# A decoder layer with expert retrieval: sums of key-score pairs on GpSimd, rows of one token tile by transposes, and the first norm's scale and shift in a later stage

## The chip, the cores and the metric

One core of a Trainium2 chip runs the whole layer in one program. The metric is the device time of that program in microseconds; the comparison is between medians of repeated runs.

## The reference

The layer works on 512 tokens with 1024 features. A mixer (pooling heads and latent attention) gives `mix`; then come two norms and a retrieval over 16384 experts. What the change touches is this (reference, cut):

```python
x  = layer_norm(ALPHA * x + g1 * mix, ln1_g, ln1_b)
h2 = x * (1.0 + sc2) + sh2
q  = (h2 @ w_peer_q).reshape(T, 8, 2, 128)            # 8 heads, two halves
sc = einsum('thpd,hpnd->thpn', q, peer_keys)          # 128 keys per half
s1, i1 = top_k(sc[:, :, 0], 16)
s2, i2 = top_k(sc[:, :, 1], 16)
cand = s1[..., :, None] + s2[..., None, :]            # sums of pairs
s, j = top_k(cand, 16)
u = peer_u[idx]; a = gelu(einsum('thkd,td->thk', u, h2))
ffn = einsum('thk,thkd->td', softmax(s) * a, peer_v[idx])
x = layer_norm(ALPHA * x + g2 * ffn, ln2_g, ln2_b)
```

## The kernel before, in words

The tokens stand in four tiles of 128 (t = 0 to 3). For tiles 0 to 2 the expert layer is computed densely over all experts: 128 **u steps** of 24 matmuls each (128 experts, three matmuls per product, since a 32-bit float is split into a high and a low half), and 128 **v steps** of 18 matmuls. Tile 3 is sparse: for each of its 128 choices a gather on the GpSimd queue (L1150) fetches one row of `peer_u` (later of `peer_v`) per token, and one VectorE instruction uses it (L1159 for u, L1172 for v, L1170 for the first v). This is the generator `sparse`.

The order of every engine's instructions is the order in which the program is written; no scheduler moves them. The stages are: mixer; first norm and transposes of h2 (`mix`, `transpose_h2`); **score stage**, the loop over m = 0 to 15 of `peer_scores`; a stage that prepares indices and gates (`top_second`, `g_tiles`); **V stage**, the loop over j = 0 to 127 of v steps with the rest of the u steps and of `sparse` between them; the end (`finish`).

*Score stage.* Iteration m multiplies h2 by the query weights `jpq[m]` in 24 matmuls (PE, L196 to L198), then multiplies the queries of m - 1 by the keys (8 matmuls, L906) and copies the scores out (ScalarE, L909). `weights` prepares the next iteration's weights: ScalarE rounds them to the high half (L208), and the low half is a subtraction, on VectorE for m up to 3 (L205) and on GpSimd after that (L203). The third matmul of an iteration (L198) is the first that reads the low half. VectorE runs `top_first(m - 1)`: the best 16 of 128 for four tiles, five operations each (L883 to L891), and at every second m `top_pairs(h)`: 16 small sums (L927) and the best 16 of the 64 pairs. In some iterations PE has matmuls of `mod_pe` (L314, L326) for the vector g2 in between. In the first four iterations `rows_out` finishes the norm of one tile on GpSimd: times gain (L778), plus bias (L779), a store of the row to DRAM (`x1d`, L780), and for tile 3 also h2 in rows (L783, L784), which `sparse` reads.

*V stage.* Per j, `v_prep` makes the halves of one block of `peer_v` (ScalarE L1214, VectorE L205) and of its weights W. After it come the steps of `sparse` that are due: `ns` counts them against a target that grows with the u and v steps done. After that, 18 matmuls. The buffers called F (17 of 128 x 1024) serve the weights, their halves, gathers and rows alike. A buffer's next user waits for its last reader.

Of the kernel before, what the change touches and what calls it, by code (L numbers as in the profile page):

```python
# [14 lines left out]
AF = mybir.ActivationFunctionType  # L15
# [5 lines left out]
P = 128  # L21
D = 1024
S = 512
NT = S // P
# [22 lines left out]
DT = 3  # L47
# [102 lines left out]
def trace(ctx: ExitStack, tc: tile.TileContext, A, out):  # L150
# [25 lines left out]
    def row(dt=F32, n=S):  # L176
        return T("S2", [P, n], dt)

    def wide(dt=F32, shape=(P, D)):
        return T("F", shape, dt)  # L180
# [9 lines left out]
    def f(t):  # L190
        return t.bitcast(F32)
# [73 lines left out]
    ident = cst[:, C_ID:C_ID + P]  # L265
# [73 lines left out]
    mods = {}  # L339
# [402 lines left out]
    xn = []  # L742
# [19 lines left out]
    for _ in mg:  # L762
        pass

    lnr = []
    hh_t = [T("H", [P, 4, S], F32R) for _ in range(2)]
    hl_t = [T("H", [P, 4, S], F32R) for _ in range(2)]
    h2h = [hh_t[k // 4][:, k % 4] for k in range(KD)]
    h2l = [hl_t[k // 4][:, k % 4] for k in range(KD)]
    x1d = [dram.tile([P, D], F32, name=f"x1d{t}") for t in range(NT)]  # L770
    h2r = {}

    def rows_out(t, xn):
        if not lnr:
            for j in range(2):
                lnr.append(wide())
                sync.dma_start(lnr[j], A["lnr"][j:j + 1].to_broadcast([P, D]))
        pool.tensor_mul(xn, xn, lnr[0])  # L778
        pool.tensor_add(xn, xn, lnr[1])  # L779
        pool.dma_start(x1d[t], xn)  # L780
        if t >= DT:
            h2r[t] = wide()
            pool.tensor_mul(h2r[t], xn, mods["sc2"])  # L783
            pool.tensor_add(h2r[t], h2r[t], mods["sh2"])  # L784

    def transpose_h2(t, xn):
        ts = slice(t * P, t * P + P)
        full = wide(shape=(P, KD, P))
        for q in range(2):
            tp = bank("tp", 2, (P, 4, P))  # L790
            for k in range(4):
                pe.transpose(tp[:, k], xn[:, (4 * q + k) * P:(4 * q + k + 1) * P], ident)
            for k in range(4):
                kk = 4 * q + k
                a, b = modc[:, 2, kk:kk + 1], modc[:, 3, kk:kk + 1]
                act.activation(full[:, kk], tp[:, k], AF.Identity, bias=b, scale=a)
            dve.tensor_copy(hh_t[q][:, :, ts], full[:, 4 * q:4 * q + 4])
            dve.tensor_sub(hl_t[q][:, :, ts], full[:, 4 * q:4 * q + 4], f(hh_t[q][:, :, ts]))


    back, bf = {}, [None]
# [43 lines left out]
            pass  # L845
        return nu[0] > n

    prev, normed = None, []
    ueng[0] = None
    for t in range(NT):  # L850
        if t >= 2:
            load_to(ju[t - 1])
        if t == 3:
            split_to(ju[1] + 1)
        last = prev
        for _ in mixes.pop(t, None) or mix(t, lambda: transpose_h2(*last), xn):
            pass
        prev = (t, xn.pop())
        normed.append(prev)
    for _ in range(2):  # L860
        u_step()
    split_to(ju[2] + 1)
# [4 lines left out]
        u_step()  # L867


    sc = []  # L870
    v16, i16, sv16, pos16 = [], [], [], []
    for t in range(NT):
        if t % 2 == 0:
            vi = wide(shape=(P, 2, 2, PH, 2, TOPK))
        v16.append(vi[:, 0, t % 2])
        i16.append(vi[:, 1, t % 2].bitcast(U32))

        sv16.append(v16[t][:, :, 0])
        pos16.append(v16[t][:, :, 1].bitcast(U32))
# [32 lines left out]
    def top_first(m):  # L912
        top16([(v16[t][:, m // 2, m % 2], i16[t][:, m // 2, m % 2], sc[m][:, t]) for t in range(NT)])

    def top_pairs(h):

        cd = (row() if h < 7 else wide())[:, :NT * 64].rearrange("p (t c) -> p t c", t=NT)
        for t in range(NT):
            for o, a0, na, nb in ((0, 0, 1, 16), (16, 1, 3, 8), (40, 4, 4, 4), (56, 8, 8, 1)):
                dst = cd[:, t, o:o + na * nb].rearrange("p (a b) -> p a b", a=na)  # L920
                s1 = v16[t][:, h, 0, a0:a0 + na].unsqueeze(2).to_broadcast([P, na, nb])
                s2 = v16[t][:, h, 1, 0:nb].unsqueeze(1).to_broadcast([P, na, nb])
                if na == 1:
                    dst, s1, s2 = dst[:, 0], s1[:, 0], s2[:, 0]
                if nb == 1:
                    dst, s1, s2 = dst[:, :, 0], s1[:, :, 0], s2[:, :, 0]
                dve.tensor_add(dst, s1, s2)  # L927
        top16([(sv16[t][:, h], pos16[t][:, h], cd[:, t]) for t in range(NT)])

    g2 = mod_pe(5 * D, "g2", dst=g2r)  # L930
    for m in range(16):
        peer_scores(m)
        if m < NT:
            rows_out(*normed[m])
        next(g2, None)
        if m:
            top_first(m - 1)
            if m % 2 == 0:
                top_pairs(m // 2 - 1)
    u_step()  # L940
    flush()
    u_step()
    top_first(15)
    top_pairs(7)
    sb_front.close()
    ps_front.close()
# [201 lines left out]
    def gather(table, k):  # L1148
        g = wide()
        pool.indirect_dma_start(out=g, out_offset=None, in_=table, in_offset=bass.IndirectOffsetOnAxis(ap=cidx[:, k:k + 1], axis=0))  # L1150
        return g

    def sparse():
        q = [gather(A["u"], k) for k in range(AHEAD - 1)]
        for k in range(P):
# [3 lines left out]
            dve.scalar_tensor_tensor(g, g, 1.0, h2r[DT], op0=ALU.mult, op1=ALU.mult, accum_out=aT[:, k:k + 1])  # L1159
            yield  # L1160
        act.activation(aT, aT, AF.Gelu)
        q = [gather(A["v"], k) for k in range(AHEAD - 1)]
        dve.tensor_mul(aT, aT, g3)
        y3 = T("Y", [P, D])
# [106 lines left out]
    for j in range(NK):  # L1271
# [7 lines left out]
        while np_[0] < j + 2 + (LAST - 1) * max(0, j + 1 + RAMP - NK) // (RAMP - LAST):  # L1279
            v_prep(np_[0])  # L1280
            np_[0] += 1
        while ns[0] < ns0 + (2 * P - ns0) * (j - 2 + nu[0] - nu0) / NJ:
            ns[0] += 1
            if next(side, 1):
                break
# [34 lines left out]
```

## Time and profile before

| | us |
|---|---|
| median of 3 runs (lowest, highest) | 1594.21 (1592.51, 1597.26) |
| profiled execution, its own time | 1597.79 |
| span of its instructions | 1595.9 |
| score stage, from its first matmul to the next u step | 125.51 |
| from there to the end of VectorE's work on scores | 24.73 |
| stage of indices and gates, to the first v matmul | 265.31 |
| V stage, to the last gap of PE | 877.22 |

The profiled execution took 1.9 us more than its span. Times within it are from the start of the span. PE is TensorE, DVE is VectorE, ACT is ScalarE, POOL is GpSimd, SP is the engine that issues most DMAs. A row of a timeline gives start, length, engine, source line, operation, what it writes and reads, and in brackets the idle time of that engine before it and what ended it. The granted clock of TensorE is given as a share of its full 2.4 GHz, so that 0.5 is 1.2 GHz.

### The profile page before, as it was taken

How to read it: one execution, taken by the hardware profiler on the slowest of the kernel's cores; microseconds unless marked ns; L12 is line 12 of the kernel's file. 1: busy time of each engine (PE TensorE's matmuls, PEld its weight loads, DVE VectorE, ACT ScalarE, POOL GpSimd, SP SyncE). 2: the span in 40 equal slices, each digit the busy share in tenths (PEclk: the TensorE clock that was granted, in tenths of full speed). 3: DMA queues.
4: the chain of work that ended last, by engine and by line, in shares of the span. 5: the costliest groups of instructions: out<-in, count | busy, mean ns of one | idle time of the engine just before them, and what ended most of it. 6: DMA issues, size and time to landing. Idle time of an engine off the chain costs nothing.

```text
span 1595.9 us, 22580 instructions
## 1 busy us (share of the span) xinstructions
PE 1504.0 (94%) x8217; PEld 1294.2 (81%) x8217; DVE 1248.0 (78%) x2717; ACT 591.4 (37%) x909; POOL 408.7 (26%) x315
## 2 busy tenths in 40 slices
PE   5999999799888989889999999999999999999996
PEld 4666678578877778769999988888888889898984
DVE  5666467689999999867687787787778778778797
ACT  3344444223333544433343333333333333333342
POOL 0001100633200000023344333342333333333313
PEclk9999999999999999989999999999999999999998
DMA  8655203443224545699889888989989889988881
GB/s 316 232 174 183 86 27 120 172 140 97 80 93 172 185 176 195 227 291 341 305 292 328 310 309 315 324 291 342 313 288 346 283 310 332 323 307 307 292 298 68
DMA packets 147296, 382.70 MB, mean 240 GB/s; under 512 B 11313, under 2 KB 62545, under 8 KB 144113
## 3 DMA queue, kind: packets, MB, share of 16 engines
q1 hardware_dynamic: 109328, 243.56, 44.2%
q0 software_dynamic: 37856, 137.70, 24.3%
q8 instruction: 64, 1.05, 0.3%
q14 instruction: 48, 0.39, 0.1%
HBM read 351.86 MB, written 29.36 MB: 239 GB/s over the span
## 4 chain that ended last, share of the span: by engine, by line
PE 67%; DVE 23%; DMA 4%; issue 2%; ACT 2%; POOL 2%; SPq 0%; DVEq 0%; POOLq 0%; ACTq 0%
PE acc L197 10%; PE acc L198 10%; PE acc L196 10%; PE a L198 9%; PE a L196 9%; PE a L197 9%; DVE F L1083 3%; DVE F L205 3%; DVE F L1087 3%; PE ps L198 2%; PE ps L197 2%; PE ps L196 2%; DVE F L1089 2%; DMA F<-in_v 1%; PE ps L671 1%
## 5 line engine op out<-in xcount | busy, mean ns | idle before, releaser
L205 DVE TENSOR_TENSOR F<-F,F 128x1024 fp32r<-128x1024 f32 (+2 forms) x274 | 334.4, 1221 | 89.6 <-ACT F L236 31.7
L198 PE MATMUL a<-H,F 128*128 128x384 f32 (+1 forms) x1040 | 355.3, 342 | 20.7 <-DVE F L205 18.4
L196 PE MATMUL a<-H,F 128*128 128x384 f32 (+1 forms) x1040 | 360.6, 347 | 2.5 <-ACT F L236 2.4
L197 PE MATMUL a<-H,F 128*128 128x384 f32 (+1 forms) x1040 | 352.1, 339 | 0.0
L1150 POOL DMA_INDIRECT F<-in_u,cidx x128 | 161.0, 1258 | 531.9 <-ACT W L1216 277.0
L196 PE MATMUL acc<-F,W 128*128 128x512 f32 x696 | 271.8, 391 | 14.2 <-ACT W L1216 14.2
L197 PE MATMUL acc<-F,W 128*128 128x512 f32 x696 | 273.3, 393 | 0.1
L198 PE MATMUL acc<-F,W 128*128 128x512 f32 x696 | 273.3, 393 | 0.0
L198 PEld LDWEIGHTS a<-H,F 128*128 128x128 f32 x1040 | 197.3, 190 | 28.1 <-DVE F L205 24.7
L1150 POOL DMA_INDIRECT F<-in_v,cidx x128 | 149.4, 1167 | 271.5 <-DVE F L205 173.2
L196 PEld LDWEIGHTS a<-H,F 128*128 128x128 f32 x1040 | 198.2, 191 | 7.4 <-ACT F L236 3.1
L1172 DVE SCALAR_TENSOR_TENSOR Y<-F,a,Y 128x1024 f32<-128x1024 f32 x127 | 162.8, 1282 | 51.7 <-DMA F<-in_v,cidx 50.2
L197 PEld LDWEIGHTS a<-H,F 128*128 128x128 f32 x1040 | 197.8, 190 | 4.2
L1159 DVE SCALAR_TENSOR_TENSOR F<-F,F 128x1024 f32<-128x1024 f32 x128 | 153.5, 1220 | 54.2 <-DMA F<-in_u,cidx 54.1
L1214 ACT ACTIVATE F<-F 128x1024 fp32r<-128x1024 f32 x128 | 134.9, 1054 | 146.1 <-DMA F<-in_v 67.1
L196 PEld LDWEIGHTS acc<-F,W 128*128 128x128 f32 x696 | 131.2, 189 | 39.8 <-ACT W L1216 14.7
L198 PEld LDWEIGHTS acc<-F,W 128*128 128x128 f32 x696 | 130.9, 188 | 27.9 <-DVE W L205 0.5
L197 PEld LDWEIGHTS acc<-F,W 128*128 128x128 f32 x696 | 131.0, 188 | 26.5 <-DVE F L205 0.9
L236 ACT ACTIVATE F<-F 128x1024 fp32r<-128x1024 f32 x120 | 126.5, 1054 | 30.5 <-DVE Y L1172 14.2
L829 ACT ACTIVATE B<-a 128x384 f32<-128x384 f32 x122 | 59.4, 487 | 210.9 <-PE a L198 210.9
L1216 ACT ACTIVATE W<-B 128x384 fp32r<-128x384 f32 x110 | 57.7, 525 | 202.9 <-PE acc L197 105.1
L198 PE MATMUL ps<-H,F 128*128 128x512 f32 x176 | 74.3, 422 | 11.5 <-POOL F L203 6.2
(284 smaller groups left out, 2041.6 us busy)
## 6 DMA issues: line engine op xcount, KB each, us to landing
F<-in_ut SPq DMA_DIRECT2D x128, 512.0 KB, 6.3
F<-in_v SPq DMA_DIRECT2D x128, 512.0 KB, 6.5
F<-in_wada SPq DMA_DIRECT2D x48, 512.0 KB, 5.1
Gd<-G SPq DMA_DIRECT2D x24, 1024.0 KB, 4.5
G<-Gd SPq DMA_DIRECT2D x15, 1536.0 KB, 13.2
F<-in_wpq SPq DMA_DIRECT2D x16, 512.0 KB, 4.4
F<-in_wout SPq DMA_DIRECT2D x8, 512.0 KB, 3.7
F<-in_win SPq DMA_DIRECT2D x8, 448.0 KB, 8.7
```

The costliest lines, as they stand in the source:

```text
L196: pe.matmul(o, lh, rh, start=first and i == 0, stop=False)
L197: pe.matmul(o, lh, rl, start=False, stop=False)
L198: pe.matmul(o, ll, rh, start=False, stop=last and i == n - 1)
L205: dve.tensor_sub(lo, src, f(hi))
L236: act.activation(hi, w, AF.Copy)
L829: act.activation(back[i], p, AF.Gelu)
L1083: dve.tensor_mul(rows(o1[:, 2:], 8), one, pairs(g[:, 1:], 8))
L1150: pool.indirect_dma_start(out=g, out_offset=None, in_=table, in_offset=bass.IndirectOffsetOnAxis(ap=cidx[:, k:k + 1], axis=0))
L1159: dve.scalar_tensor_tensor(g, g, 1.0, h2r[DT], op0=ALU.mult, op1=ALU.mult, accum_out=aT[:, k:k + 1])
L1172: dve.scalar_tensor_tensor(y3, g, aT[:, k:k + 1], y3, op0=ALU.mult, op1=ALU.add)
L1214: act.activation(Vhl[j][0], v, AF.Copy)
L1216: act.activation(W[j][0], w, AF.Copy)
```

## The change

Three parts.

1. `rows_out` goes. The unscaled normed rows are stored to `x1d` as soon as a tile's norm is done (GpSimd queue, L854 of the new file). Gain and bias are applied in the V stage, inside `sparse`, between the last u and the first v: two loads of gain and bias, then for each tile a load of the row, a multiplication, an addition and a store, all on GpSimd, one tile per step. The target of `ns` counts 4 steps more.
2. The h2 rows of tile 3 are made in `transpose_h2`, by transposing the 8 blocks of h2 back on TensorE and copying them out on ScalarE.
3. The pair sums are done for two tiles at a time (8 instructions per head where there were 16), on GpSimd for heads 0 to 6, at the even m before the odd m at which their best 16 are taken; those of head 7 stay on VectorE.

```diff
-        pool.tensor_mul(xn, xn, lnr[0])
-        pool.tensor_add(xn, xn, lnr[1])
-        pool.dma_start(x1d[t], xn)
-        if t >= DT:
-            h2r[t] = wide()
-            pool.tensor_mul(h2r[t], xn, mods["sc2"])
-            pool.tensor_add(h2r[t], h2r[t], mods["sh2"])
...
+        if t >= DT:
+            h2r[t] = wide()
+            for q in range(2):
+                tp = bank("tp", 2, (P, 4, P))
+                for k in range(4):
+                    pe.transpose(tp[:, k], full[:, 4 * q + k], ident)
+                act.activation(h2r[t][:, q * S:(q + 1) * S], tp.rearrange("p a b -> p (a b)"), AF.Copy)
...
+        pool.dma_start(x1d[t], prev[1])
...
+    def pair_sums(h, eng):
+        cands[h] = (row() if h < 7 else wide())[:, :NT * 64].rearrange("p (t c) -> p t c", t=NT)
+        for t in range(0, NT, 2):
+            for o, a0, na, nb in ((0, 0, 1, 16), (16, 1, 3, 8), (40, 4, 4, 4), (56, 8, 8, 1)):
...
+                eng.tensor_add(dst, s1.to_broadcast(dst.shape), s2.to_broadcast(dst.shape))
...
         peer_scores(m)
-        if m < NT:
-            rows_out(*normed[m])
         next(g2, None)
         if m:
             top_first(m - 1)
             if m % 2 == 0:
+                pair_sums(m // 2 - 1, pool)
+            elif m > 1:
                 top_pairs(m // 2 - 1)
...
     top_first(15)
+    pair_sums(7, dve)
     top_pairs(7)
...
         act.activation(aT, aT, AF.Gelu)
+        h2r.pop(DT)
+        l1 = [wide() for _ in range(2)]
+        for j in range(2):
+            pool.dma_start(l1[j], A["lnr"][j:j + 1].to_broadcast([P, D]))
+        for t in range(NT):
+            x = wide()
+            pool.dma_start(x, x1d[t])
+            pool.tensor_mul(x, x, l1[0])
+            pool.tensor_add(x, x, l1[1])
+            pool.dma_start(x1d[t], x)
+            yield
+        del l1, x
         q = [gather(A["v"], k) for k in range(AHEAD - 1)]
...
-        while ns[0] < ns0 + (2 * P - ns0) * (j - 2 + nu[0] - nu0) / NJ:
+        while ns[0] < ns0 + (2 * P + NT - ns0) * (j - 2 + nu[0] - nu0) / NJ:
```

How the order of the engines' instructions moves, at two places.

GpSimd in the score stage, before. L203 is the low half of the next weights, the rest are rows_out of tiles 0 to 3:

```order
L779 TENSOR_TENSOR F_1912<-F_1912,F_2260 128x1024
L780 DMA x1d_1768<-F_1912 128x1024
L203 TENSOR_TENSOR F_2442<-F_2268,F_2441 128x1024
L778 TENSOR_TENSOR F_2014<-F_2014,F_2258 128x1024
L779 TENSOR_TENSOR F_2014<-F_2014,F_2260 128x1024
L780 DMA x1d_1769<-F_2014 128x1024
L783 TENSOR_TENSOR F_2484<-F_2014,F_967 128x1024
L784 TENSOR_TENSOR F_2484<-F_2484,F_1325 128x1024
L203 TENSOR_TENSOR F_2516<-F_2335,F_2515 128x1024
L203 TENSOR_TENSOR F_2617<-F_2439,F_2616 128x1024
```

The same queue now. F_2238 and F_2239 hold the best 16 that VectorE found, S is the buffer of the 64 sums, and the L203 behind them is the low half of the weights of iteration 4:

```order
L854 DMA x1d_1769<-F_2017 128x1024
L922 TENSOR_TENSOR S_485_2406<-F_2238 128x2x16
L922 TENSOR_TENSOR S_485_2406<-F_2238 128x2x24
L922 TENSOR_TENSOR S_485_2406<-F_2238 128x2x16
L922 TENSOR_TENSOR S_485_2406<-F_2238 128x2x8
L922 TENSOR_TENSOR S_485_2406<-F_2239 128x2x16
L922 TENSOR_TENSOR S_485_2406<-F_2239 128x2x24
L922 TENSOR_TENSOR S_485_2406<-F_2239 128x2x16
L922 TENSOR_TENSOR S_485_2406<-F_2239 128x2x8
L203 TENSOR_TENSOR F_2418<-F_2278,F_2417 128x1024
L203 TENSOR_TENSOR F_2506<-F_2342,F_2505 128x1024
```

The rows_out work is gone from the queue, and eight sums of a head stand ahead of every second L203; the pattern comes seven times.

GpSimd in the V stage now, from the last gather of `peer_u` on:

```order
L1149 DMA F_10372<-in_u,cidx 128x1024
L1164 DMA F_10440<-in_lnr 128x1024
L1164 DMA F_10441<-in_lnr 128x1024
L1167 DMA F_10444<-x1d_1766 128x1024
L1168 TENSOR_TENSOR F_10444<-F_10444,F_10440 128x1024
L1169 TENSOR_TENSOR F_10444<-F_10444,F_10441 128x1024
L1170 DMA x1d_1766<-F_10444 128x1024
L1167 DMA F_10511<-x1d_1767 128x1024
L1168 TENSOR_TENSOR F_10511<-F_10511,F_10440 128x1024
L1169 TENSOR_TENSOR F_10511<-F_10511,F_10441 128x1024
```

Two more tiles follow in the same way, and only then the first gathers of `peer_v` (F_10555, F_10557, F_10561). Before, these gathers stood right behind the last gather of `peer_u`. The buffers of the two L1164 loads are those of F_10331 and F_10330, halves of a v block that PE reads last in the v step ahead of the u step a_10403.

VectorE at the same place now:

```order
L205 TENSOR_TENSOR F_10505<-F_10394,F_10504 128x1024
L205 TENSOR_TENSOR W_10503<-B_8561,W_10502 128x384
L1226 TENSOR_TENSOR B_8664<-B_8664,G_9702 128x384
L205 TENSOR_TENSOR F_10549<-F_10467,F_10548 128x1024
L205 TENSOR_TENSOR W_10547<-B_8664,W_10546 128x384
L1174 TENSOR_TENSOR a_3936<-a_3936,g_3934 128x128
L1181 TENSOR_SCALAR Y_10560<-F_10555,a_3936 128x1024
L205 TENSOR_TENSOR F_10589<-F_10398,F_10588 128x1024
L1226 TENSOR_TENSOR B_8734<-B_8734,G_9702 128x384
```

L1181 uses the first gather of `peer_v`, F_10555; the low half F_10589 of a u step's weights stands behind it. That u step on PE now:

```order
L196 MATMUL acc_6848<-F_10548,W_10546 128x512
L197 MATMUL acc_6848<-F_10549,W_10546 128x512
L198 MATMUL acc_6848<-F_10548,W_10547 128x512
L196 MATMUL a_10661<-H_1762,F_10588 128x384
L197 MATMUL a_10661<-H_1764,F_10588 128x384
L198 MATMUL a_10661<-H_1762,F_10589 128x384
```

Between the last read of F_10331 and F_10330 and the u step a_10661 stand 144 matmuls on PE: three u steps and four v steps.

## Rows read from the trace of the kernel before

**Rows 1.** Busy time by stretch: limits, length, each engine's busy us (instructions), clock, DMA share, GB/s.

```profile
273.73:399.24 125.51, 113.12 (x542) 90.50 (x541) 102.03 (x731) 30.72 (x45) 57.24 (x27) 0.95 0.44 143
423.97:689.28 265.31, 227.19 (x1969) 203.91 (x1968) 244.19 (x518) 115.77 (x187) 0.00 (x0) 0.95 0.50 175
689.28:1566.50 877.22, 875.90 (x4323) 783.18 (x4321) 682.67 (x862) 317.94 (x429) 316.66 (x259) 1.00 0.88 309
1000.00:1200.00 200.00, 200.00 (x994) 179.70 (x993) 154.94 (x204) 72.26 (x98) 73.95 (x61) 1.00 0.90 312
```

**Rows 2.** Timeline of PE in the score stage.

```profile
284.65 1.05 PE L906 MATMUL ps<-S,S 128*128 128x128 f32 x8
...
298.97 0.80 PE L198 MATMUL ps<-H,F 128*128 128x512 f32 x1 [5.29 <-DVE F L205]
...
321.59 0.79 PE L198 MATMUL ps<-H,F 128*128 128x512 f32 x1 [6.20 <-POOL F L203]
...
350.97 1.05 PE L906 MATMUL ps<-S,S 128*128 128x128 f32 x8
...
357.31 1.05 PE L906 MATMUL ps<-S,S 128*128 128x128 f32 x8
...
364.91 1.05 PE L906 MATMUL ps<-S,S 128*128 128x128 f32 x8
```

**Rows 3.** Timeline of GpSimd ahead of the second of these waits.

```profile
319.19 2.34 POOL L203 TENSOR_TENSOR F<-F,F 128x1024 fp32r<-128x1024 f32 x1
```

**Rows 4.** Chain of work that ended last, VectorE in the score stage: start, us, what.

```profile
348.23 0.76 DVE F L883 x4
...
357.57 1.35 DVE S L927 x16
358.93 0.51 DVE F L883 x4
...
362.28 0.76 DVE F L883 x4
```

**Rows 5.** Timeline of VectorE: start of the first best-16, end of the scores.

```profile
286.49 0.87 DVE L883 MAX8 F<-S 128x8 f32<-128x128 f32 x4 [2.67 <-DMA x1d<-F]
...
423.97 0.20 DVE L1043 CAST iotab<-cst 128x128 bf16<-128x128 f32 x1
```

**Rows 6.** Groups of instructions, GpSimd and VectorE: count, busy us, mean ns, idle before.

```profile
L203 POOL TENSOR_TENSOR F<-F,F 128x1024 fp32r<-128x1024 f32 x18 | 43.0, 2389 | 76.8 <-ACT F L208 31.7 <-issue 12.9 <-PE ps L197 11.2
L203 POOL TENSOR_TENSOR S<-F,S 128x512 fp32r<-128x512 f32 x4 | 5.2, 1314 | 62.3 <-ACT S L208 62.3
L297 POOL COPY cz<-cact 128x8 f32<-128x8 f32 x2 | 0.3, 192 | 0.1
...
L205 DVE TENSOR_TENSOR F<-F,F 128x1024 fp32r<-128x1024 f32 x256 | 315.1, 1232 | 77.4 <-ACT F L236 31.7 <-ACT F L1214 30.4 <-ACT F L208 7.6
```

**Rows 7.** DMA issues: count, KB of one, median us to landing.

```profile
F<-in_v SPq DMA_DIRECT2D x128, 512.0 KB, 6.5
x1d<-F POOLq DMA_DIRECT2D x4, 512.0 KB, 3.1
F<-in_v,cidx POOLq DMA_INDIRECT x128, 7.4
```

**Rows 8.** Timeline of PE at two shorter waits.

```profile
419.71 0.69 PE L198 MATMUL a<-H,F 128*128 128x384 f32 x1 [2.04 <-POOL F L203]
...
560.27 0.45 PE L198 MATMUL a<-H,F 128*128 128x384 f32 x1 [2.23 <-DVE F L205]
```

**Rows 9.** Busy time in short stretches that begin with these waits' ends.

```profile
419.63:423.04 3.41, 3.33 (x10) 3.33 (x11) 3.41 (x36) 0.00 (x0) 0.02 (x1) 0.50 0.02 5
...
560.27:563.70 3.43, 3.43 (x35) 3.18 (x36) 3.40 (x8) 0.60 (x1) 0.00 (x0) 1.00 0.74 306
```

**Rows 10.** Timeline at the transposes of tile 3: PE, ScalarE.

```profile
269.17 0.42 PE L196 MATMUL a<-H,F 128*128 128x384 f32 x1
...
269.32 2.89 ACT L796 ACTIVATE F<-ps,modc 128x128 f32<-128x128 f32 x8
```

More of the change, by code (lines that the diff above doesn't have):

```diff
@@ L763, in trace @@
         pass
-    lnr = []
     hh_t = [T("H", [P, 4, S], F32R) for _ in range(2)]
@@ L771, in trace @@
     h2r = {}
[L773 to L777, printed above, removed]
-        pool.tensor_mul(xn, xn, lnr[0])
-        pool.tensor_add(xn, xn, lnr[1])
-        pool.dma_start(x1d[t], xn)
-        if t >= DT:
-            h2r[t] = wide()
-            pool.tensor_mul(h2r[t], xn, mods["sc2"])
-            pool.tensor_add(h2r[t], h2r[t], mods["sh2"])
     def transpose_h2(t, xn):
@@ L846, in u_step @@
         return nu[0] > n
-    prev, normed = None, []
+    prev = None
     ueng[0] = None
@@ L858, in trace @@
         prev = (t, xn.pop())
-        normed.append(prev)
+        pool.dma_start(x1d[t], prev[1])
     for _ in range(2):
@@ L867, in trace @@
         u_step()
-    sc = []
+    sc, vis, cands = [], [], {}
     v16, i16, sv16, pos16 = [], [], [], []
@@ L874, in trace @@
             vi = wide(shape=(P, 2, 2, PH, 2, TOPK))
+            vis.append(vi)
         v16.append(vi[:, 0, t % 2])
@@ L913, in top_first @@
         top16([(v16[t][:, m // 2, m % 2], i16[t][:, m // 2, m % 2], sc[m][:, t]) for t in range(NT)])
-    def top_pairs(h):
[L917 to L927, printed above, removed]
+    def pair_sums(h, eng):
+        cands[h] = (row() if h < 7 else wide())[:, :NT * 64].rearrange("p (t c) -> p t c", t=NT)
+        for t in range(0, NT, 2):
+            for o, a0, na, nb in ((0, 0, 1, 16), (16, 1, 3, 8), (40, 4, 4, 4), (56, 8, 8, 1)):
+                v = vis[t // 2][:, 0, :, h]
+                dst = cands[h][:, t:t + 2, o:o + na * nb]
+                s1, s2 = v[:, :, 0, a0:a0 + na], v[:, :, 1, 0:nb]
+                if na > 1 and nb > 1:
+                    dst = dst.rearrange("p t (a b) -> p t a b", a=na)
+                    s1, s2 = s1.unsqueeze(3), s2.unsqueeze(2)
+                eng.tensor_add(dst, s1.to_broadcast(dst.shape), s2.to_broadcast(dst.shape))
+    def top_pairs(h):
+        cd = cands.pop(h)
         top16([(sv16[t][:, h], pos16[t][:, h], cd[:, t]) for t in range(NT)])
```

## Prediction

> **What bounds the kernel now.** I read the table of stretches first. In the V stage PE is busy for 875.9 of 877.2 us while DVE is busy for 78% of it [rows 1]: PE sets its length, and work added to another engine costs nothing there unless PE comes to wait for it. In the stage of indices and gates DVE is busy for 244 of 265 us and PE for 227 [rows 1], so that stage starts when DVE is done with the scores (423.97 [rows 5]) and shifts with that moment. The score stage has no single bound: PE 113 and DVE 102 of 125.5 us [rows 1]. Its timelines say what happens in it. Undisturbed, an iteration on PE takes 6.34 us, and a pair 13.94 where matmuls for g2 stand between (L906 at 350.97, 357.31, 364.91 [rows 2]); four such groups and two smaller ones lie in the stage, about 1 us each, so 16 x 6.34 + 6 = 107.4 us, a mean of 13.4 a pair. The stage took 18.1 us more. Two waits of PE explain it: 5.29 us for an L205 whose buffer was held by a row that rows_out had not yet stored, and 6.20 us for an L203 that stood behind rows_out on GpSimd [rows 2, 3]; the remaining 6.6 us are a short wait before them and the slower clock after each. From then on the chain of waits runs on DVE: a pair of iterations costs it 14.05 us, 9.35 for two best-16 (4.67 each), 1.36 for 16 sums, 3.35 for the best 16 of the pairs [rows 4]. DVE is the later of the two by a little, and ends 24.7 us after PE has left the scores.
>
> **Part 1, what is removed and moved in the score stage.** rows_out goes from GpSimd, and the two waits of PE with it: -18.1 us for PE. The stores at L854 are issued before the stage and stand ahead of nothing urgent. The 16 sums leave DVE for heads 0 to 6: -1.36 us a pair for DVE, which would then need 12.7 a pair and no longer bind against PE's 13.4.
>
> **Part 2, transposes.** PE now turns tile 3 back before it may go on to the u step at 269.17. These transposes need ScalarE's eight outputs, 2.89 us from 269.32, ending at 272.2 [rows 10], and about 0.5 us of their own. PE leaves at 272.7 instead of 269.2: +3.5 us. The two copies on ScalarE are hidden; nothing waits for h2 in rows before the V stage. The scores begin at 273.7 + 3.5 = 277.2.
>
> **Part 3, pair sums on GpSimd: a new loop.** This is the first place where I expect a cost. In the new order eight sums stand ahead of every second L203. They wait for DVE's best-16 of m - 1, that waits for the key matmuls, which stand at the end of iteration m on PE; and PE's iteration m + 2 waits for that L203. One turn of the loop, from the third matmul of iteration m to that of m + 2:
>
> - rest of the 24 matmuls after the third: 22 x 0.227 = 5.0 us;
> - key matmuls, copy, start of DVE: 286.49 - 284.65 = 1.84 [rows 2, 5];
> - best-16 of m - 1 on DVE: 4.67 [rows 4];
> - eight sums on GpSimd: X;
> - L203: 2.39 [rows 6], and 0.3 for the hand-overs (PE started 0.06 us after L203's end [rows 2, 3]).
>
> That is 14.2 + X, against 13.4 that PE needs. X has no row. GpSimd takes 1.314 us for 512 columns and 2.389 for 1024 [rows 6], so 2.1 ns a column and 0.24 us an instruction: eight instructions with 256 columns in all give 2.5 us. The lower bound is eight times its smallest copy, 0.192: 1.5; above, I allow 0.5 us each for broadcast operands: 4. I take 2.5, from the same operation. So PE waits about 3 us at every second iteration. Waits of that size were followed by half clock once and not another time (2.04 us, then 0.50; 2.23 us, then 1.00 [rows 8, 9]); being longer here, I count 3.4 us at half clock after each, which delays the matmuls in the loop by 1.5 us. A turn is then 18.2 us.
>
> The Trainium skill (GPSIMD Engine Reference, Engine selection) advises VectorE for two-input elementwise work and gives GpSimd about twice its time. By that estimate, from DVE's 0.7 us for eight sums, X would be 1.4 and the score term below some 8 us better; no run here shows X.
>
> In order: iteration 2 starts at 277.2 + 11.7 (two iterations with one group of key matmuls) and ends 6.34 us later; DVE begins on the scores of m = 1 1.03 us after that (1.84 less the key matmuls' share) and takes 4.67; sums 2.5, L203 and hand-overs 2.6: iteration 4 has its low half at 306.1, where PE would have been at 303.1. Five more turns bring iteration 14, and a sixth the u step behind the scores, whose L203 also stands behind sums: 306.1 + 6 x 18.2 = 415.3. From there 3.7 us for its matmuls, 1.84 for the last scores, then on DVE 4.67, 0.7 (the eight sums of head 7) and 3.35: 429.6 against 423.97, **+6 us**. Without slow clock it is -3; with X of 1.5 in addition -10, with X of 4 and slow clock +16. So the stage, freed of 18 us, is about as long as before: the removed wait is replaced by a new one.
>
> **Part 4, gain and bias in the V stage.** 256 steps become 260; the extra work is off PE and DVE, and 5 MB more in 877 us at 309 GB/s [rows 1] is 2% of the traffic. What counts is the order. GpSimd does load, multiply, add, store for four tiles one after the other and only then issues the first gather of `peer_v`. DVE waits for that gather at L1181, and behind L1181 stands the L205 for a u step (F_10589). From the moment E at which PE frees the two gain and bias buffers:
>
> - both loads and the first row issued at 0.6 us each, the row landing 6.5 us after its issue (the same size in this stage [rows 7]): E + 7.7;
> - two GpSimd operations of 2.39 [rows 6] with gaps 4.9, store 0.6: E + 13.2;
> - three more tiles, each 6.5 + 4.9 + 0.7 = 12.1, the next load being behind the store: E + 49.5;
> - first gather, 7.4 to landing [rows 7]: E + 56.9;
> - L1181 and L205, 2 us at L205's price with the first a little shorter [rows 6]: E + 58.9.
>
> Up to the third matmul of that u step PE has 146 matmuls, at 200 / 994 us each [rows 1] 29.4 us. So PE **stands for 29.5 us**, in a stage where it stood nowhere; with the slow clock after it (2 x 2.85 us followed the two long waits above: 18.1 less 11.5 and 0.9) **+32 us**. Nothing gives it back: the remaining matmuls are as many as before. DVE's own lead covers none of it, since its instructions are in order. The bounds: with every landing at 3.1 us, as the stores in a quiet stage took [rows 7], the gather comes at E + 38 and the cost is +15; with landings of 9 us, +45.
>
> The row's 3.1 us was in a stage with a DMA share of 0.44, and the loads at 6.5 and 7.4 were in one of 0.88 [rows 1, 7]; I go by the latter. The Trainium skill (DMA: Bandwidth & Descriptors, Anatomy of one DMA) gives a DMA from this queue 2.0 us plus its bytes at 436 GB/s, an estimate of 3.2 us for one row tile, and by it the cost would be the lower bound, +15. The stores' 3.1 us agrees with it, the loads of the V stage do not.
>
> **Sum.** +6 and +32 make +38 us. The profiled execution took 1597.8 by its own time, so 1635.8; the median of the runs is 3.6 us lower, which gives **1632 us**. The extremes are -10 + 15 and +16 + 45 on 1594: 1599 to 1655.
>
> **The rivals.**
>
> *The scores gain, the V stage loses* (chance 0.16). If the sums don't hold L203, PE leaves the scores at 277.2 + 107.4 = 384.6 and DVE is done 17.7 us later (a start of 1.0, then two best-16, two of pairs and the last sums), at 402.3: -22. With +32 that is 1604. For it: GpSimd was idle for more than half of that stage [rows 1]. Against it: idle time doesn't help a loop, and even X = 0 leaves 14.2.
>
> *Faster: gain and bias stay hidden, too* (0.07). The same -22 and 0 from the V stage: 1572. It takes GpSimd being through four tiles and a gather within 29.4 us of E, or being 30 us ahead of PE; the first asks for 1 us or less a landing, the second for free buffers that the program hasn't given. The first gather's time against 29.4 us decides.
>
> *No difference* (0.07): the V stage at its lower bound of +15 and the scores at -10 to -20, within 0.3% (4.8 us, about what a measurement here can tell from none).
>
> *Worse than the forecast* (0.08): X near 4, or landings that queue behind three loads at once: above 1650.
>
> **Numbers.** The forecast, both new waits with about their prices, has 0.62, and stretches from 1616 to 1650. To leave out no more than two in ten the range reaches down to the first rival: 1604 to 1650. Slower is 0.62 + 0.16 + 0.08 = 0.86, same 0.07, faster 0.07.
>
> **What would show it.** Right: PE in the V stage shows one idle gap of 20 to 40 us that ends at an L205 or L1181 on DVE, released by the first gather of `peer_v`, and it is the only one; in the score stage PE waits at L198 for GpSimd's L203 at iterations 4, 6, ... 14, some 3 to 5 us each, and the waits behind rows_out are gone; DVE ends the scores within 10 us of 424; PE leaves tile 3's transposes 3.5 us later. Wrong: no gap in the V stage, or eight sums in under 1 us and a score stage that ends 20 us earlier.

## The result, and the profile after

The changed kernel takes 1607.05 us (median of 5 runs, 1605.43 to 1611.10) against 1594.61 us of the kernel before in runs beside it: a ratio of 1.0078, 95% interval 1.0066 to 1.0091. It is 12.4 us slower, where 1632 was forecast: the direction is right, the size is a third. The profiled execution took 1606.82 us by its own time with a span of 1605.1, so 9.2 us over the span of before; it is less than 12.4 because the profiled execution of the kernel before, 1597.79 us, lay 3.2 us above the median of its runs.

Where the 9.2 us are can be read from four moments. In the kernel before they are 423.97 (VectorE done with the scores [rows 5]), 685.54 (first matmul of the V stage), 1582.37 (its last) and 1595.9 (end). Now they are 410.27, 671.71, 1591.84 and 1605.1.

| part | before | after | difference |
|---|---|---|---|
| up to the end of the scores on VectorE | 423.97 | 410.27 | -13.7 (forecast +6) |
| indices and gates, to the first matmul of the V stage | 261.57 | 261.44 | -0.1 |
| V stage, first to last matmul | 896.83 | 920.13 | +23.3 (forecast +32) |
| end | 13.5 | 13.3 | -0.3 |

The table ahead of the prediction cuts the V stage at 689.28 and 1566.50; here it is counted from its first matmul to its last. The busy time by stretch (limits, length, then PE, weight loads, DVE, ACT, POOL with their counts, clock, DMA share, GB/s), cut as in [rows 1], with the end of the score stage in a row of its own:

```profile
277.89:389.19 111.30, 109.04 (x542) 86.54 (x541) 89.70 (x644) 30.49 (x45) 39.31 (x66) 1.00 0.38 118
389.19:410.10 20.91, 18.55 (x102) 17.94 (x101) 19.31 (x138) 8.50 (x12) 11.55 (x8) 0.92 0.26 76
410.10:675.45 265.35, 228.81 (x1992) 205.86 (x1991) 244.99 (x520) 115.92 (x187) 0.96 (x1) 0.96 0.50 175
675.45:1576.50 901.05, 876.90 (x4322) 784.41 (x4320) 684.67 (x862) 317.12 (x429) 348.90 (x277) 0.99 0.88 307
```

PE stood for 12.4 us of the score stage before and stands for 2.3 now; in the V stage it is the reverse, 1.3 us and 24.

**The score stage.** First the timeline of PE, then GpSimd's and VectorE's, over one turn of the loop:

```profile
304.43 0.50 PE L198 MATMUL ps<-H,F 128*128 128x512 f32 x1
...
309.56 1.05 PE L902 MATMUL ps<-S,S 128*128 128x128 f32 x8
...
318.81 0.50 PE L198 MATMUL ps<-H,F 128*128 128x512 f32 x1 [0.20 <-POOL F L203]
...
361.78 0.50 PE L198 MATMUL ps<-H,F 128*128 128x512 f32 x1 [1.33 <-POOL F L203]
...
392.13 0.69 PE L198 MATMUL a<-H,F 128*128 128x384 f32 x1 [2.36 <-POOL F L203]
```

```profile
314.79 1.64 POOL L922 TENSOR_TENSOR S<-F 128x32 f32<-128x32 f32 x8 [7.51 <-DVE F L885]
316.38 2.37 POOL L203 TENSOR_TENSOR F<-F,F 128x1024 fp32r<-128x1024 f32 x1
```

```profile
311.37 0.86 DVE L879 MAX8 F<-S 128x8 f32<-128x128 f32 x4
...
314.22 0.87 DVE L885 MAX8 F<-S 128x8 f32<-128x128 f32 x4
315.00 0.08 DVE L887 MATCH_VALUE_LOAD F<-F,S 128x8 f32 x1
```

The turn is there in the forecast order: third matmul of an iteration (304.43), key matmuls (309.56), VectorE's best 16 (from 311.37), GpSimd's sums (314.79), L203 (to 318.75), third matmul two iterations later (318.81). It takes 14.38 us where the forecast had 18.2, and PE hardly waits: 0.20 us here, later 1.33, 0.38 and 2.36 us. The six turns from 304.43 to 392.13 take 14.62 us on average, four of them 14.3 to 14.4 and the last two 15.1 and 15.2.

**The V stage.** PE's only long gap, and what VectorE did then:

```profile
1149.53 0.69 PE L198 MATMUL a<-H,F 128*128 128x384 f32 x1 [23.91 <-DVE F L205]
```

```profile
1147.59 0.75 DVE L1181 TENSOR_SCALAR Y<-F,a 128x1024 f32<-128x1024 f32 x1 [31.66 <-DMA F<-in_v,cidx]
1148.26 1.22 DVE L205 TENSOR_TENSOR F<-F,F 128x1024 fp32r<-128x1024 f32 x1
```

GpSimd ahead of it: the loads of gain and bias, load and multiplication of the first tile and of the second, the multiplication of the fourth, and the first gather. Additions and stores lie between them.

```profile
1096.35 1.14 POOL L1164 DMA_DIRECT2D F<-in_lnr  x2 [7.00 <-PE acc L198]
1097.47 0.55 POOL L1167 DMA_DIRECT2D F<-x1d  x1
1105.18 2.64 POOL L1168 TENSOR_TENSOR F<-F,F 128x1024 f32<-128x1024 f32 x1 [7.17 <-DMA F<-x1d]
...
1111.37 0.54 POOL L1167 DMA_DIRECT2D F<-x1d  x1
1116.23 2.39 POOL L1168 TENSOR_TENSOR F<-F,F 128x1024 f32<-128x1024 f32 x1 [4.32 <-DMA F<-x1d]
...
1137.01 2.33 POOL L1168 TENSOR_TENSOR F<-F,F 128x1024 f32<-128x1024 f32 x1 [4.31 <-DMA F<-x1d]
...
1142.94 1.00 POOL L1149 DMA_INDIRECT F<-in_v,cidx  x1 [0.30 <-issue]
```

It is the forecast chain, place by place: the buffers come free at E = 1096.35 with PE's last read, PE has 29.27 us of matmuls left (forecast 29.4), and its u step waits for the L205 behind L1181 behind the first gather. The chain takes 53.2 us instead of 58.9.

### The profile page after: what moved, and what is told of

Same layout as the page of the kernel before. It is cut to its first block, busy times and chain, and to the rows that moved or that the text cites. A ratio compares the mean times of both kernels' runs of the same rounds, so it can differ in the third digit from the quotient of the medians.

```text
span 1605.1 us, 22565 instructions
## 1 busy us (share of the span) xinstructions
PE 1499.9 (93%) x8225; PEld 1290.6 (80%) x8225; DVE 1234.8 (77%) x2597; ACT 592.1 (37%) x911; POOL 428.1 (27%) x379
## 4 chain that ended last, share of the span: by engine, by line
PE 52%; DVE 14%; DMA 4%; POOL 1%; issue 1%; ACT 1%; SPq 0%; POOLq 0%; DVEq 0%; ACTq 0%
PE acc L197 10%; PE acc L198 10%; PE acc L196 10%; PE a L198 8%; PE a L196 8%; PE a L197 7%; DVE F L1082 3%; DVE F L205 3%; DVE F L1086 3%; DVE F L1088 2%; DMA F<-in_v 2%; DMA F<-x1d 1%; PE gp L1095 1%; POOL F L1168 1%; POOL F L1169 1%
## 5 line engine op out<-in xcount | busy, mean ns | idle before, releaser
L205 DVE TENSOR_TENSOR F<-F,F 128x1024 fp32r<-128x1024 f32 (+2 forms) x274 | 332.9, 1216 | 86.4 <-ACT F L1225 30.1
L1149 POOL DMA_INDIRECT F<-in_v,cidx x128 | 158.7, 1240 | 240.9 <-DVE F L205 129.4
L196 PEld LDWEIGHTS acc<-F,W 128*128 128x128 f32 x696 | 131.1, 188 | 39.4 <-ACT W L1227 14.2
L1095 PE MATMUL gp<-F 128*128 128x128 bf16 x1152 | 81.8, 220 | 2.0 <-DVE F L1088 1.9
```

The source lines that it names most:

```text
L196: pe.matmul(o, lh, rh, start=first and i == 0, stop=False)
L205: dve.tensor_sub(lo, src, f(hi))
L1095: pe.matmul(p[:, j], o[:, 0, j], o[:, n, j], start=n == 2, stop=n == 1)
```

## The experiments

Kernels of one group ran beside their own runs of the kernel before, whose median lay between 1594.05 and 1597.61. Moments are from the profiled executions. A time without a ratio beside it is that of a single run. "Gap" is a wait of PE.

### The loop in the score stage

**Sums one iteration later.** `pair_sums` goes to the odd m, behind the L203 that PE needs next.

```diff
         if m:
+            if m > 1 and m % 2:
+                pair_sums(m // 2 - 1, pool)
             top_first(m - 1)
-            if m % 2 == 0:
-                pair_sums(m // 2 - 1, pool)
-            elif m > 1:
+            if m > 1 and m % 2:
                 top_pairs(m // 2 - 1)
```

> The changed kernel with the pair sums of a head issued on GpSimd one iteration later, behind the low half of the next weights. Theory (a loop PE - VectorE - GpSimd's sums - low half - PE sets 14.35 us a pair of iterations): the waits of PE at the third matmul of every second iteration go, a pair takes PE's own 13.4, the wait of 2.36 us at the u step behind the scores goes with its slower clock, and VectorE ends the scores at 402 to 406 instead of 410.3; the median falls by 4 to 8 us, the gap in the V stage stays at 24. Rival (VectorE is the bound again, as before the change): VectorE ends within 2 us of 410 and the median stays.

1599.15 us, ratio to before 1.0019 (1.0010 to 1.0029). VectorE ends the scores at 401.94, PE has no wait at an L203 in the score stage, the gap in the V stage stays (23.87). So the order on GpSimd's queue costs the change 8 us.

**Twice the sums.** Each of GpSimd's sums is issued twice.

> The changed kernel with every pair sum on GpSimd done twice (same result). Theory (the eight sums lie in the loop): seven times 1.6 us more ahead of the low half, a pair takes 16 us instead of 14.35, and VectorE ends the scores 9 to 16 us later, more if the clock falls in the longer waits; the time rises by about as much, to 1616 or above. Rival (GpSimd's sums are beside the path): VectorE ends within 2 us of 410 and the time stays at 1607.

1636.34 us; VectorE ends at 436.81, 26.5 us later, and more than expected. PE's waits, and the busy time of the 3.4 us right behind each of the first four:

```profile
306.50 0.80 PE L198 MATMUL ps<-H,F 128*128 128x512 f32 x1 [2.64 <-POOL F L203]
326.31 0.79 PE L198 MATMUL ps<-H,F 128*128 128x512 f32 x1 [2.72 <-POOL F L203]
344.76 0.50 PE L198 MATMUL ps<-H,F 128*128 128x512 f32 x1 [2.66 <-POOL F L203]
361.61 0.50 PE L198 MATMUL ps<-H,F 128*128 128x512 f32 x1 [2.66 <-POOL F L203]
...
378.45 0.80 PE L198 MATMUL ps<-H,F 128*128 128x512 f32 x1 [3.85 <-POOL F L203]
...
398.89 0.80 PE L198 MATMUL ps<-H,F 128*128 128x512 f32 x1 [2.93 <-POOL F L203]
...
418.53 0.69 PE L198 MATMUL a<-H,F 128*128 128x384 f32 x1 [3.97 <-POOL F L203]
```

```profile
306.45:309.86 3.41, 3.35 (x8) 2.68 (x9) 3.41 (x31) 0.00 (x0) 2.33 (x2) 0.50 0.66 184
...
326.30:329.70 3.40, 3.39 (x8) 2.71 (x9) 3.40 (x32) 0.00 (x0) 2.28 (x1) 0.51 0.62 174
...
344.70:348.10 3.40, 3.34 (x15) 2.76 (x16) 3.40 (x31) 0.00 (x0) 2.37 (x2) 1.00 0.11 37
361.60:365.00 3.40, 3.40 (x15) 2.82 (x16) 3.40 (x32) 0.00 (x0) 2.30 (x1) 1.00 0.11 40
```

With 16 sums of 4.2 us instead of 8 of 1.64 a turn takes 19.8 and 18.5 us at first: half clock (0.5 of 2.4 GHz) follows the first two waits. From 344.76 to 361.61, where the clock stays at 1.00, a turn is 16.85, which is 14.38 and the 2.56 us that the sums are longer, to 0.1. Behind each of the last three waits the clock is at 0.50 for 3.4 us, and the last two turns take 20.4 and 19.6 us. Those turns at half clock are the regime that the forecast described; only X has to be 4.2 for it.

**All sums on VectorE**, still for two tiles at a time, at the place of the change:

```diff
-                pair_sums(m // 2 - 1, pool)
+                pair_sums(m // 2 - 1, dve)
```

> The changed kernel with the sums of all heads on VectorE, still for two tiles at a time (8 instructions a head), at the same place of the program. Theory (the turn of 14.35 us runs through GpSimd's sums and the L203 behind them; VectorE alone needs 9.35 + 0.7 + 3.35 = 13.4 a pair): L203 no longer waits for VectorE, a pair of iterations takes 13.4 to 13.6 us, and VectorE ends the scores at 402 to 405, as with the sums one iteration later: about 1600. Rival (VectorE's load is what sets the pace and GpSimd relieves it): VectorE ends 0.7 us a head later than in the changed kernel, at about 415, and the time is 1611 or more.

1602.93 us, ratio 1.0038 (1.0026 to 1.0050). Two iterations take 13.94 us with a g2 group between (L902 at 302.39 and 316.33), as undisturbed before [rows 2]; VectorE ends at 404.82. GpSimd isn't needed for the sums: with half as many instructions (0.90 us for eight, 1.35 for sixteen [rows 4]) VectorE keeps PE's pace.

**Transposes back behind the last two u steps** ahead of the scores (`turn_back` after them, on the kept `full`).

> The changed kernel, with the eight transposes back and their two copies moved behind the last two u steps ahead of the score stage. Theory (PE stands for ScalarE's eight outputs, two waits of 1.39 and 0.74 us, and does nothing else wrong): the waits go, the scores begin at 275 to 276 instead of 277.9, everything behind them is some 2 to 2.7 us earlier: about 1604. Rival (the transposes themselves, about 1 us, are the whole price and the waits only move): the start of the scores stays within 0.7 us of 277.9 and the time within 1 us of the changed kernel's.

The scores begin at 273.94; the waits of 1.39 and 0.74 us at L791 are gone, and VectorE ends at 406.57. The V stage begins 3.2 us earlier (668.53), and the time, 1605.73 us, is 1.3 us below the change's median, which a single run cannot tell from none.

### The gap in the V stage

**All loads first.** The four rows are loaded right behind gain and bias into four buffers, before the first multiplication.

> The changed kernel with the four rows of x1d loaded at once ahead of the first multiplication, so that only the first landing stands in GpSimd's chain. Theory (the gap is GpSimd's chain less PE's 29 us of work): three landings of about 4.9 us with their issue leave the chain, the gap shrinks from 23.9 to 8 to 12 us and the time by as much, to about 1593. Rival (the operations on GpSimd, not the landings, hold VectorE through the port that they share): the gap changes by less than 4 us.

1595.70 us; the gap:

```profile
1138.96 0.69 PE L198 MATMUL a<-H,F 128*128 128x384 f32 x1 [10.03 <-DVE F L205]
```

13.9 us less than in the change, with the same operations and the same bytes: those were the landings of tiles 1 to 3 in a row, 14.3 us in the change.

**Spread over the v half.** One piece (load; multiplication; addition and store) after every fourth v step of `sparse`, so that no gather waits for the chain.

> The changed kernel with gain and bias spread between the v steps of the sparse tile: every fourth step one piece (loads, multiplication, addition and store apart), so that GpSimd never waits for a landing ahead of a gather. Theory (order: VectorE waits for the first gather of peer_v, which stands behind four tiles in GpSimd's queue): the one gap of 23.9 us in the V stage goes, that stage takes 877 to 880 us instead of 901, the median falls by 22 to 25 us to about 1583, 0.7% below the kernel before. Rival (the extra traffic and GpSimd's operations cost the time, wherever they stand): the V stage stays at 895 or more, in many small gaps, and the median above 1600.

1605.76 us, ratio 1.0058 (1.0037 to 1.0079): no better. The long gap is gone, but three waits sum to 10.6 us (3.84 us at 1174.81, 2.65 at 1200.49, 4.11 at 1288.01), and the V stage takes 914.6; with the clock at 0.50 to 0.62 behind each of these waits, PE's busy time is 6.8 us longer as well. My first reading was that a buffer given up by a store still under way held up a low half. **One buffer for all rows**, kept from the first load to the last store, should have ended that:

> The changed kernel with gain and bias in the V stage as in the spread version, but with one buffer for all four rows, one piece at every second step, and a piece left empty between a store and the next load into the same buffer; it starts at the sixth step of the v half. Theory (the spread version lost what it won because a buffer given up by a store still under way went to a low half for PE a few us later, and the gathers behind it were late in turn): with the buffer kept, that can happen only once, after the last store; the waits of PE in the V stage sum to 0 to 4 us, and the stage from its first v matmul to its last comes near the 896.8 us it took before the change (894 to 902): 1582 to 1588. Rival (three buffers less for 100 us or more are the cause): waits like those of the spread version (11 to 12 us in all), about 1598 to 1606.

1603.04 us, ratio 1.0049 (1.0033 to 1.0064); waits of 9.11 us at 1201.48 and 1.49 at 1272.53, V stage 913.2. The reading falls; the time is what the rival, three buffers less, expected. What happened before the 9.11 us, on GpSimd and on VectorE:

```profile
1178.27 2.40 POOL L1174 TENSOR_TENSOR F<-F,F 128x1024 f32<-128x1024 f32 x1
...
1186.00 1.06 POOL L1149 DMA_INDIRECT F<-in_v,cidx  x1 [4.46 <-DVE F L205]
```

```profile
1177.82 3.94 DVE L1191 SCALAR_TENSOR_TENSOR Y<-F,a,Y 128x1024 f32<-128x1024 f32 x1
...
1196.72 1.28 DVE L1191 SCALAR_TENSOR_TENSOR Y<-F,a,Y 128x1024 f32<-128x1024 f32 x1 [8.02 <-DMA F<-in_v,cidx]
```

L1191, else 1.28 us, took 3.94 beside GpSimd's L1174. And the next gather was issued only when a VectorE instruction had freed a buffer, so that its landing lay open. Two more kernels, which leave gain and bias out of the computation, part the two: **without the operations** (loads, stores and held buffers stay) and **the operations alone** (on one buffer of zeros, no loads or stores).

> The spread version with one row buffer, without its eight operations on GpSimd: gain and bias are left out of the computation, rows are loaded and stored unchanged, and the three buffers are held just as long. If the missing buffers are what costs in the spread versions: PE waits in the V stage for about 11 us as with the operations. If the operations are (a VectorE instruction that meets one of them takes up to 2.7 us longer, the gathers behind it are late in turn): 0 to 2 us of waits, and a V stage of 894 to 898 us.

> The spread version with one row buffer, with its eight GpSimd operations on a buffer of zeros at the same places: no loads, no stores, one buffer held instead of three; gain and bias are left out of the computation. If the buffers and DMAs are what costs: 0 to 2 us of waits of PE in the V stage, which takes 894 to 898 us. If the operations are: 8 to 12 us of waits as in the spread version.

Without operations: one wait of 5.83 us, the others 0.53 or less, V stage 906.7, 1594.64 us. Operations alone: one of 1.67 us, V stage 899.4, 1587.06 us. Against the 896.8 of before, buffers and DMAs cost 9.9 us, the operations 2.6, and both together 16.4. Buffers and DMAs are the larger part, but not the whole. That the two do more than add is not shown: each length is from one execution, and the operations on zeros, with a single input buffer, took 16.1 us in all where those of the version with one row buffer took 20.9.

**In the stage of indices**, where GpSimd has nothing to do [rows 1] and buffers can be spared (a piece at every second step of `g_tiles`):

> The changed kernel with gain and bias in the stage of indices and gates, one piece (load; multiplication; addition and store) at every second step of it, instead of in the V stage. Theory (what costs in the V stage is only that the first gather of the v rows stands behind a chain of landings): the gap of 23.9 us in the V stage is gone with nothing in its place, since no F buffer is held there and GpSimd has nothing to do in the stage of indices; that stage grows by 0 to 3 us; VectorE ends the scores near 410 as before: 1582 to 1587. Rival (GpSimd's eight operations of 2.4 us share the memory port with VectorE, which sets the pace of that stage): the stage grows by up to 19 us, from 265 to 280 or more, and the time is 1597 to 1602.

1602.55 us, ratio 1.0037 (1.0026 to 1.0047). The V stage is down to 894.1 with no gap, but the stage of indices takes 284.7 instead of 261.4 us. VectorE and GpSimd there:

```profile
471.64 0.68 DVE L1099 TENSOR_TENSOR F<-F,gp 128x1024 bf16<-128x1024 bf16 x1
472.24 2.84 DVE L1103 TENSOR_TENSOR F<-iotab,sm 128x1024 bf16<-128x1024 bf16 x1
475.01 2.56 DVE L1105 TENSOR_TENSOR F<-F,gp 128x512 bf16<-128x512 bf16 x1
```

```profile
472.18 2.35 POOL L1079 TENSOR_TENSOR F<-F,F 128x1024 f32<-128x1024 f32 x1 [6.58 <-DMA F<-x1d]
474.61 2.67 POOL L1081 TENSOR_TENSOR F<-F,F 128x1024 f32<-128x1024 f32 x1
```

Operations of 0.68 and 0.42 us take 2.84 and 2.56, each until GpSimd's is over. GpSimd's eight operations, 21.3 us in all, add 17.7 us to VectorE's busy time in that stage (241.1 to 258.8); the other 5.5 us are idle time of VectorE whose cause is not shown. The rival holds, with 23 us where it had 19: the stage in which GpSimd was idle is the dearest place. The Trainium skill (SBUF — State Buffer, SBUF: two separate sides) says that VectorE and GpSimd share one port pair as an exclusive lock, held for a whole instruction; this trace agrees: L1103 and L1105 end 0.5 and 0.3 us after the operations that they met.

**At the end.** The rows are loaded once, for the second norm, and GpSimd multiplies and adds in that buffer:

```diff
     def load_ln2(ts):
...
+        for t in ts:
+            pool.tensor_mul(x1s[t], x1s[t], ln2[2])
+            pool.tensor_add(x1s[t], x1s[t], ln2[3])
```

> The changed kernel with gain and bias at the end of the program instead of in the middle of the V stage: rows are loaded once, as they are for the second norm anyway, and GpSimd multiplies and adds in that same buffer (tile 3 after the last gather, tiles 0 to 2 while the last v steps run); the four extra loads and four stores of rows are gone, two buffers more are held for some 30 us. Theory (the gap is only the first gather behind the chain; GpSimd is idle after its last gather at 1541 and VectorE uses the rows from 1561 and 1579 on): no gap in the middle of the V stage, the stage takes 894 to 899 us, the tail is 0 to 4 us longer: 1582 to 1587. Rival (buffers, as in the spread versions, or VectorE waiting for the rows of tile 3, or the last norms waiting for GpSimd's six operations at the end): waits of 5 us or more in the last 60 us, 1590 or more.

1598.85 us, ratio 1.0016 (1.0004 to 1.0027). No gap until 1549; then eight waits between 0.2 and 2.4 us, 13.3 in all, beside GpSimd's operations, as VectorE's timeline there shows:

```profile
1549.51 2.70 DVE L205 TENSOR_TENSOR B<-B,B 128x384 fp32r<-128x384 f32 x1
1552.13 0.55 DVE L1216 TENSOR_TENSOR B<-B,G 128x384 f32<-128x384 f32 x1
1552.60 3.59 DVE L205 TENSOR_TENSOR F<-F,F 128x1024 fp32r<-128x1024 f32 x1
```

An L205 of 0.55 us takes 2.70, one of 1.22 takes 3.59: the rival again, and these rows point to the port rather than to the buffers, though the two were not parted here.

**Quarters from one buffer.** One buffer holds 256 columns of gain, of bias and of a row tile; a piece at every third step over most of the v half, 32 operations on 256 columns.

```diff
+            gb = wide(shape=(P, 4, D // 4))
+            g, b, x = gb[:, 0], gb[:, 1], gb[:, 2]
+            for c in range(4):
+                cs = slice(c * D // 4, (c + 1) * D // 4)
...
+                for t in range(NT):
+                    pool.dma_start(x, x1d[t][:, cs])
+                    yield
+                    pool.tensor_mul(x, x, g)
+                    pool.tensor_add(x, x, b)
+                    pool.dma_start(x1d[t][:, cs], x)
+                    yield
```

> The changed kernel with gain and bias in the V stage, worked off in quarters of 256 columns from one buffer that holds a quarter of the gain, of the bias and of one row tile; one piece (load; or multiplication, addition, store) at every third step, so over most of the v half. Theory (in the spread versions two missing buffers more and VectorE instructions held up to 2.7 us by an operation of 2.4 us made the remaining waits): one buffer is held instead of three and each operation is a quarter as long, so PE's waits in the V stage sum to 0 to 2 us and the stage takes 895 to 899 us: 1583 to 1588, about what the run with the operations alone took (1587). Rival (32 more DMAs on GpSimd's queue and 32 operations hold up the gathers): waits of 5 us or more, 1592 or more.

1586.03 us, ratio 0.9947 (0.9925 to 0.9968). V stage 899.2, waits of PE 0.98, 0.35 and 0.53 us: as expected, and what the operations alone took. The operations are shorter and the buffers fewer at the same time; which of the two did it was not parted.

### All three edits

Sums one iteration later and transposes behind the u steps, with gain and bias in the stage of indices, spread with one row buffer, at the end, or in quarters:

> The three edits together: sums on GpSimd one iteration later, transposes back behind two u steps, gain and bias in the stage of indices. Theory (three separate waits, whose prices add): 1607 less 8 (sums), less 2 to 3 (transposes), less 21 to 25 (gain and bias) = 1571 to 1576, 18 to 23 us faster than the kernel before. Rival (what is gained ahead of the stage of indices is lost in it, or GpSimd's work there slows VectorE): 1585 or more.

> The same, and with it the sums on GpSimd one iteration later and the transposes back behind the last two u steps. Theory (the three waits are separate): 1607 less 8 less 2 less 20 to 24: 1573 to 1578. Rival (buffers): 1587 or more.

> The same, with the sums on GpSimd one iteration later and the transposes back behind the last two u steps. Theory (three separate waits): 1607 less 8 less 2 less 20 to 25 = 1572 to 1577, 1.1 to 1.4 per cent faster than the kernel before. Rival (as for gain and bias at the end alone): 1580 or more.

> The same, with the sums on GpSimd one iteration later and the transposes back behind the last two u steps. Theory: 1583 to 1588 less 8 less 1 to 3 = 1573 to 1578, about 1.2 per cent faster than the kernel before. Rival: as for the version in quarters alone, or the wait of 5.2 us that came at the start of the stage of indices in the earlier versions with all three edits: 1579 to 1583.

1591.17, 1587.71, 1588.03 and 1576.25 us; ratios 0.9964 (0.9951 to 0.9976), 0.9965 (0.9952 to 0.9977), 0.9944 (0.9930 to 0.9959) and 0.9892 (0.9873 to 0.9912). The first three miss what was expected by about what their places for gain and bias cost; the last meets it. Its V stage, first to last matmul:

```profile
659.29:1555.73 896.44, 894.27 (x4392) 797.39 (x4392) 713.75 (x894) 323.49 (x435) 404.20 (x333) 1.00 0.88 309
```

896.4 against the 896.8 of before, with VectorE done with the scores at 397.60 instead of 423.97: the three parts of the change are worth 1.1% when they make PE wait for almost nothing in the scores and in the V stage. The wait at the start of the stage of indices that the expectation names is there (5.26 us at 426.56), but costs nothing: that stage, which VectorE bounds, takes 261.7 us as before (261.6).

## Why the prediction was wrong

- **Part 1, removal of rows_out: right.** Its two long waits are gone, and PE's iterations run at 6.34 us wherever it doesn't wait.
- **Part 2, transposes: right.** The scores begin at 277.89 (forecast 277.2); moving the transposes away takes the wait with it.
- **Part 3, the new loop: the mechanism was right, the sizes were not, and this is the step that failed.** The forecast turn was 14.2 + X with X = 2.5, and 1.5 for half clock: 18.2 us. Term by term, in the turn shown above: 22 matmuls 5.0, measured 5.13; key matmuls and copy 1.84, measured 1.81; best 16 on VectorE 4.67, measured 3.42; X 2.5, measured 1.59 to the start of L203; L203 and hand-overs 2.7, measured 2.43; half clock 1.5, measured 0. The 4.67 was the length of a whole best-16 group. The sums read only its values, not the indices, so they begin while L885 still works on the last tiles, and the search L887 (1.0 us) is no part of the loop. X was taken from large operations by the column and by the instruction; it stood near its lower bound.

  So the score stage gained 13.7 us, more than the forecast's own extreme of -10. The difference between +6 and -13.7, part by part: the first low half on GpSimd comes at 304.43 where 306.1 was forecast, 1.7 us earlier; the six turns take 87.7 us instead of 109.2, 21.5 less; from there to the end of the scores it is 18.14 us instead of 14.26, 3.9 more. Of these, 2.4 us are the last eight sums on VectorE, 3.12 us where 0.7 was counted (0.90 when all sums are on VectorE), beside an L203 of GpSimd:

```profile
403.88 3.12 DVE L922 TENSOR_TENSOR F<-F 128x32 f32<-128x32 f32 x8
```

```profile
404.35 2.51 POOL L203 TENSOR_TENSOR F<-F,F 128x1024 fp32r<-128x1024 f32 x1 [1.39 <-DVE F L887]
```

  The other 1.5 come from the half clock behind the wait at 392.13 (3.4 us at 0.50). That shorter waits then bring no half clock within the turns is why the error is larger than the two sizes alone: 14.62 is only 1 us above what PE needs by itself (13.4 forecast; 13.6 for the same six turns with the sums one iteration later), while the doubled sums, at X = 4.2, bring back both the waits and, in most turns, the clock.
- **The first rival came near by luck.** It had a chance of 0.16, with -22 for the scores and +32 for the V stage, +10 in all. Measured are -13.7 and +23.3: each of its terms is 8 to 9 us off, and the errors cancel. Its condition, that the sums don't hold L203, isn't met in the change either; with the sums one iteration later it is, and the scores end where it had them (401.94; it had 402.3).
- **Part 4, V stage: place and mechanism right, the term too large** (+32, measured +23.3, within its bounds; by its own terms the gather of the lower bound comes at E + 39, not 38). The landings of tiles 1 to 3 were priced at 6.5 us and the gather at 7.4, as in the running stage. The first load, issued while PE still ran and right behind the loads of gain and bias, took 7.71 us at a DMA share of 0.90; those after it, as the stage ran dry, 4.57 to 4.86, and the gather 4.65, at 0.63 and then 0.38. The rows for it, and the 3.4 us behind the gap:

```profile
1097.47:1105.18 7.71, 7.71 (x41) 6.97 (x40) 5.64 (x8) 3.74 (x6) 0.55 (x2) 1.00 0.90 331
1111.37:1126.00 14.63, 14.25 (x69) 12.25 (x67) 1.90 (x3) 1.96 (x3) 6.43 (x6) 1.00 0.63 218
1126.00:1149.50 23.50, 0.00 (x0) 0.00 (x0) 1.91 (x3) 1.06 (x1) 16.04 (x12) 0.56 0.38 128
1149.53:1152.95 3.42, 3.42 (x11) 3.42 (x12) 3.38 (x5) 2.79 (x4) 0.00 (x0) 0.50 0.97 318
```

  The landings shorten as the traffic falls; that the one is the reason for the other is read from these rows, not tried by itself. The slow clock, forecast at 2.85 us, fell almost wholly into the gap and lasted 3.4 us behind it (about 1.7 us of delay, an estimate: half of that). What the forecast left out is the price of GpSimd's operations for VectorE ("off PE and DVE"). In the V stage of the change VectorE stood anyway, so it doesn't show; the versions that put whole-row operations beside a working VectorE meet it. The trace of before has it, too: an L205, else 1.23 us, beside an L779.

```profile
280.99 2.83 DVE L205 TENSOR_TENSOR F<-F,F 128x1024 fp32r<-128x1024 f32 x1 [6.19 <-ACT F L208]
```

```profile
280.35 2.39 POOL L779 TENSOR_TENSOR F<-F,F 128x1024 f32<-128x1024 f32 x1 [0.28 <-DMA F<-in_lnr]
```

- **The sum.** -13.7 and +23.3 make +9.6 where +6 and +32 made +38. Both terms erred the same way, and the time is longer than before because the V stage lost more than the scores gained. The measured 1607 lies below the forecast's band (1616 to 1650); the range has it only because it was stretched down to the first rival.

## What to carry to other kernels

Cut a loop across engines at the instruction that produces the value, not at the end of the group in which it stands, and price small operations by small ones: errors of 0.9 and 1.3 us a turn decided here between waits of 3 us with half clock behind them and hardly any wait. Work moved to an idle engine costs what it shares with the busy one: see which buffers it holds, for how long, and which port, before its own time; short operations from one buffer cost 2.4 us of the V stage, where the same work in three buffers cost 16 and beside a VectorE at its limit 23. Price a transfer at the traffic of its own moment: the DMA share was 0.90 for the first load here and 0.38 for the last.

## What the runs showed of the hardware

- Eight two-input operations of 16 to 48 columns take 1.64 us on GpSimd, 0.2 us each, against 0.90 on VectorE.
- A VectorE instruction that met an operation of GpSimd of 2.35 to 3.2 us took 1.6 to 2.7 us longer than elsewhere, 32-bit subtractions (L205) as well as bf16 operations (L1103, L1105); VectorE's eight sums for head 7 (3.12 us) and L1191 in the V stage of the spread version (3.94) are of the same kind.
- Half clock followed some waits of about 2.4 to 2.7 us and not others: the 2.36 us at 392.13 in the changed kernel came with 3.4 us at 0.50, of the seven waits in the doubled sums two of 2.66 us were followed by full clock and those of 2.64, 2.72, 2.93, 3.85 and 3.97 by half clock. Up to 2.7 us, length alone doesn't tell.
